# A hybrid decoder layer: output projection's tiles in four steps, FFN's first sums on VectorE, gate weight splits spread over the down projection

## The chip, the cores and the metric

One core of a Trainium2 chip runs the whole layer. The time is device microseconds of one execution, from launch to the output in memory. Lower is better. A time stands for the median of several executions; the profile is of one further execution.

Names used below: TensorE (PE) does matmuls and transposes, VectorE (DVE) and ScalarE (ACT) elementwise work, GpSimd (POOL) elementwise work too, and SyncE (SP) issues nearly all transfers, in one queue. On-chip memory is cut into two areas, mem_r (72 units, for operands of matmuls) and mem_f (30 units, for everything else); a unit is 512 floats in each of 128 partitions. PSUM has 8 banks of the same size.

## What is computed

The reference is a decoder layer for 1024 tokens of width 1024, in float32. Cut to what matters here:

```python
h = rmsnorm(x, mix_pre_norm)
z = h @ w_in
a = mla(z[..., :o1], z[..., o1:o2], z[..., o2:o3], ...)      # 8 heads, causal
c = short_gated_conv(z[..., o3:o4], z[..., o4:o5], z[..., o5:], conv_w)
m = concatenate([rmsnorm(a, attn_group_norm), rmsnorm(c, conv_group_norm)])
x = x + rmsnorm(m @ w_out, mix_post_norm)                    # output projection
h = rmsnorm(x, ffn_pre_norm)
f = (silu(h @ w_gate) * (h @ w_up)) @ w_down                 # FFN, width 2816
x = x + rmsnorm(f, ffn_post_norm)
e = rmsnorm(p @ w_ple_proj, ple_norm)
x = x + sigmoid(x @ w_ple_gate) * e                          # gate
```

## The kernel before

**Arithmetic.** Every float32 operand of a matmul is split into a high part (a cast on ScalarE, line 197) and a low part (the operand less its high part, on VectorE, line 198). A product is then three matmuls: high by high, high by low, low by high (lines 208 to 210, 1123 to 1126, 1281 to 1283). The three large products of FFN and of the gate use a scheme with seven block products in place of eight: blocks of the operands are first added to and subtracted from one another, then split, and seven products are summed into four blocks. The order of the seven is ORDER = 1, 2, 6, 5, 7, 3, 4. On the side of the activations the right operands are B11, B21 and B22 (plain blocks of the normed rows) and T1 to T4 (sums of blocks). Products 1 and 2 need B11 and B21 alone, which come from the first four row tiles.

**Output projection** (wo_a, lines 999 to 1019). There are eight tiles of 128 tokens. The convolution's half of the product, y, was stored to memory before (wo_c, line 941). For a tile, wo_a loads the rows of x and of y (lines 1001, 1002), makes the attention half with 24 matmuls into two banks (wo_half), adds y (line 1004), squares on ScalarE with a sum (line 218), adds epsilon on VectorE (line 214) and takes the power -1/2 on GpSimd (line 215), multiplies by that and the gain (line 1010), adds x (line 1011; on GpSimd in tiles 2, 4 and 6, by XP), stores the new residual row x1 (line 1013), and does the same norm once more into a third buffer, n1 (lines 1015 to 1017). Then h2_turn (line 1028) transposes n1 on TensorE, 8 transposes into 2 banks, copies them on ScalarE, and splits them: both halves for the first four tiles (B11, B21), one for the last four (B22). For the first four tiles the plain transposed copy is stored to memory too (hr_d, line 1048); for the last four it stays on the chip as tr[0] and tr[1]. The loop (line 1185) writes wo_a(t) and behind it h2_turn(t-1). The buffers of two units come from the first 22 units of mem_f (ML), of which the weights loaded ahead (line 1180) take two buffers.

**Start of FFN** (lines 1189 to 1223). FF is cut in 11 pairs of 128 columns each, fp; m is 0 for w_gate and 1 for w_up. `factor(fp, m, p)` (line 1082) makes the weight's operand for product p: for p = 6, 5, 7 and 3 of blocks that GpSimd adds (lines 1093, 1094, 1099, 1102), and splits it. `product` (line 1113) does the 12 matmuls and brings the result out of PSUM. The first four products (fp 0, p 1 and 2, m 0 and 1) are written around the last transposes; then the T's are made: lines 1206 and 1207 on VectorE, lines 1208 and 1216 on GpSimd, each 128x2048, each followed by a cast and a split of that size; then the products 1 and 2 of fp 1, and the loop over the rest, in which factor runs five products ahead (AHEAD). w_factors (line 1165) makes sums of w_down for the next stage on GpSimd.

**Down projection** (lines 1411 to 1434). 77 steps: f_load (two blocks), f_split (two splits), down (12 matmuls). Meanwhile wg_factors(k) (line 1302) prepares w_ple_gate: for each of four k two loads of 512 KB, seven splits and four GpSimd sums, called whole at four steps, 22, 17, 12 and 7 ahead of the last eleven.

**What sets the order.** The program is written as one sequence; a planner (the last lines, schedule_with_timeline_sim) then orders each engine's instructions, with modelled times and the written order as priority, and sets the waits. Each engine runs its own queue in that order. Buffers are chosen when the program is written: of those that are free, the one freed longest ago. A transfer into a buffer waits for the last reader of it.

Of the kernel before, what the change touches and what calls it, by code (L numbers as in the profile page):

```python
# [132 lines left out]
def hybrid_layer(ctx: ExitStack, tc: tile.TileContext, x, x_t, p_t, cols_in, positions,  # L133
# [36 lines left out]
    RG = ((56, 72),)  # L170
    ML, MG, MW = ((0, 22),), ((18, 22),), ((0, 8),)
# [759 lines left out]
    x1n = {}  # L931
# [66 lines left out]

    def wo_a(t):
        xr, y = mf(2, ML), mf(2, ML)  # L1000
        sp.dma_start(xr.a, x[t * P : (t + 1) * P, :])
        sp.dma_start(y.a, y_d[t * P : (t + 1) * P, :])
        ids, b = wo_half(t, mTa, 0)
        dve.scalar_tensor_tensor(y.a, b, ss_a[:, t : t + 1], y.a, op0=ALU.mult, op1=ALU.add)  # L1004
# [5 lines left out]
        dve.scalar_tensor_tensor(y.a, y.a, r, g_mix.a, op0=ALU.mult, op1=ALU.mult)  # L1010
        (pool if t in XP else dve).tensor_tensor(y.a, y.a, xr.a, op=ALU.add)
# [5 lines left out]
        dve.scalar_tensor_tensor(n1.a, y.a, r, g_ffn.a, op0=ALU.mult, op1=ALU.mult)
        free(y)
        x1n[t] = n1
# [8 lines left out]
    def h2_turn(t):  # L1028
        src = x1n.pop(t)
# [149 lines left out]

    raw_load(0, 0, MW)  # L1180
    for p in (1, 2):
        for m in range(2):
            factor(0, m, p)
    tr[0], tr[1] = mf(4, ((22, 26),)), mf(4, ((26, 30),))
    for t in range(T):
        wo_a(t)
        if t > 0:
            h2_turn(t - 1)
    for d in (mTa, wo):
        for h, l in d.values():  # L1190
            free(h, l)
    free(g_mix, g_ffn)
    head = [(0, m, p) for p in (1, 2) for m in range(2)]
# [302 lines left out]
```

## Time and profile before

| | |
|---|---|
| runs before | 1266.06, 1266.36 and 2819.84 us; median 1266.36 |
| profiled execution | 1260.9 us, span on the core 1259.1 us |
| mean granted TensorE clock | 0.986 |
| busy: PE, DVE, ACT, POOL | 1205.3, 823.3, 586.8, 544.6 us |
| moved by DMA | 215.68 MB, mean 171 GB/s |
| stages in the span | attention and what comes before it to about 440 us; output projection to 527; FFN's first products to 955; down projection, then the gate to the end |

The third run of those before stands alone, and the median is not moved by it. In the page, a group of instructions has its line, engine and operation, what it writes and reads, how often it ran, its busy time and the mean of one in ns. A row of the timeline gives start and length in us, and in brackets how long the engine stood idle before it and what ended that. In the busy time by stretch, PE's column is matmuls (their ends are modelled, they overlap), and the granted clock is 1.00 at full speed and 0.50 at half.

### The profile page before, as it was taken

What the parts mean: (1) busy time and instruction counts of PE and PEld (TensorE: products, weight loads), DVE (VectorE), ACT (ScalarE), POOL (GpSimd) and SP (SyncE); (2) the same over time, 40 slices, a digit from 0 to 9 for tenths busy, and PEclk for the clock granted to TensorE, in tenths of its full rate; (3) what the DMA queues carried; (4) which work ended last, traced back from release to release, by engine and by line L of the source; (5) the groups of instructions that cost most, each with busy time, mean ns of one, the idle gap of its engine ahead of it and who ended that gap; (6) DMA issues with size and microseconds to landing.
All of it is one profiled execution on the core that took longest, in us unless ns stands there. A gap on an engine that the chain in (4) does not pass through costs nothing.

```text
span 1259.1 us, 16644 instructions
## 1 busy us (share of the span) xinstructions
PE 1205.3 (96%) x5902; PEld 1012.9 (80%) x5902; DVE 823.3 (65%) x1158; ACT 586.8 (47%) x1071; POOL 544.6 (43%) x404
## 2 busy tenths in 40 slices
PE   7899999999999998769999999999999999989998
PEld 6898888888999886548888888888887888768886
DVE  7955457388867566697575564756535454889775
ACT  6542423277766644543333343333334445566552
POOL 5523544235634222277965665766611000442321
PEclk9999999999999998879999999999999999999999
DMA  7523554994541846435644445543337665566332
GB/s 244 171 67 109 184 185 162 285 336 115 137 104 56 284 161 209 159 109 184 234 163 143 147 157 184 176 167 139 137 126 277 199 190 186 180 222 234 118 128 82
DMA packets 88943, 215.68 MB, mean 171 GB/s; under 512 B 8920, under 2 KB 17404, under 8 KB 87548
## 3 DMA queue, kind: packets, MB, share of 16 engines
q1 hardware_dynamic: 88800, 214.60, 51.5%
q8 instruction: 46, 0.75, 0.3%
q14 instruction: 39, 0.30, 0.1%
q10 hardware_dynamic: 58, 0.02, 0.0%
HBM read 143.28 MB, written 71.04 MB: 170 GB/s over the span
## 4 chain that ended last, share of the span: by engine, by line
PE 80%; DVE 8%; DMA 6%; issue 2%; ACT 2%; POOL 1%; SPq 0%; DVEq 0%; ACTq 0%; POOLq 0%
PE banks L1125 11%; PE banks L1123 11%; PE banks L1126 11%; PE banks L208 7%; PE banks L210 7%; PE banks L209 7%; DVE mem_r L198 4%; PE banks L1282 4%; PE banks L1281 4%; PE banks L1283 4%; PE banks L843 2%; PE banks L1384 2%; PE banks L1381 2%; PE banks L1383 2%; PE banks L814 1%
## 5 line engine op out<-in xcount | busy, mean ns | idle before, releaser
L198 DVE TENSOR_TENSOR mem_r<-mem_f,mem_r 128x512 fp32r<-128x512 f32 (+3 forms) x401 | 397.1, 1019 | 211.9 <-ACT mem_r L197 200.0
L197 ACT CAST mem_r<-mem_f 128x512 fp32r<-128x512 f32 (+1 forms) x404 | 258.7, 669 | 402.5 <-PE banks L1125 160.9
L1123 PE MATMUL banks<-mem_r 128*128 128x512 f32 x616 | 244.0, 397 | 10.6 <-DVE mem_f L1004 7.0
L1125 PE MATMUL banks<-mem_r 128*128 128x512 f32 x616 | 243.6, 396 | 8.7 <-DVE mem_r L198 8.7
L1126 PE MATMUL banks<-mem_r 128*128 128x512 f32 x616 | 243.2, 395 | 0.0
L208 PE MATMUL banks<-mem_r 128*128 128x512 f32 (+2 forms) x536 | 196.3, 373 | 4.6 <-DVE mem_f L1004 3.3
L209 PE MATMUL banks<-mem_r 128*128 128x512 f32 (+2 forms) x536 | 197.1, 369 | 1.0 <-DVE mem_r L201 0.7
L210 PE MATMUL banks<-mem_r 128*128 128x512 f32 (+2 forms) x536 | 196.5, 368 | 0.0
L1123 PEld LDWEIGHTS banks<-mem_r 128*128 128x128 f32 x616 | 118.0, 191 | 37.2 <-issue 7.4
L1125 PEld LDWEIGHTS banks<-mem_r 128*128 128x128 f32 x616 | 117.8, 191 | 34.1 <-DVE mem_r L198 9.6
L1126 PEld LDWEIGHTS banks<-mem_r 128*128 128x128 f32 x616 | 117.9, 191 | 25.2
L1282 PE MATMUL banks<-mem_r 128*128 128x512 f32 x308 | 120.7, 392 | 7.5 <-DVE mem_r L198 7.5
L1281 PE MATMUL banks<-mem_r 128*128 128x512 f32 x308 | 119.2, 390 | 1.2 <-ACT mem_r L197 1.2
L1283 PE MATMUL banks<-mem_r 128*128 128x512 f32 x308 | 119.0, 389 | 0.0
L208 PEld LDWEIGHTS banks<-mem_r 128*128 128x128 f32 x536 | 100.9, 190 | 22.0 <-DVE mem_f L1004 3.9
L209 PEld LDWEIGHTS banks<-mem_r 128*128 128x128 f32 x536 | 101.6, 190 | 17.5 <-DVE mem_r L201 1.2
L210 PEld LDWEIGHTS banks<-mem_r 128*128 128x128 f32 x536 | 101.3, 189 | 16.3
L828 POOL TENSOR_TENSOR mem_f<-mem_f,stats 128x640 f32<-128x640 f32 (+5 forms) x64 | 72.5, 1147 | 92.6 <-DVE stats L827 46.7
L1141 DVE TENSOR_TENSOR mem_f<-banks,mem_f 128x512 f32<-128x512 f32 x66 | 45.3, 687 | 67.0 <-PE banks L1126 66.8
L215 POOL TENSOR_TENSOR small<-small,mhalf 128x1 f32<-128x1 f32 (+2 forms) x42 | 39.1, 930 | 114.6 <-DVE small L214 112.0
L198 DVE TENSOR_TENSOR mem_r<-banks,mem_r 128x512 fp32r<-128x512 f32 (+3 forms) x118 | 69.2, 611 | 10.5 <-ACT mem_r L197 9.7
L1282 PEld LDWEIGHTS banks<-mem_r 128*128 128x128 f32 x308 | 57.8, 188 | 22.0 <-DVE mem_r L198 10.4
(190 smaller groups left out, 1910.4 us busy)
## 6 DMA issues: line engine op xcount, KB each, us to landing
sc_d<-mem_f SPq DMA_DIRECT2D x77, 256.0 KB, 3.1
mem_f<-sc_d SPq DMA_DIRECT2D x77, 256.0 KB, 2.8
mem_f<-in_w_up_dram SPq DMA_DIRECT2D x22, 512.0 KB, 4.1
mem_f<-in_w_gate_dram SPq DMA_DIRECT2D x22, 512.0 KB, 4.6
mem_f<-in_w_down_dram SPq DMA_DIRECT2D x22, 512.0 KB, 4.6
wc_d<-mem_f SPq DMA_DIRECT2D x22, 512.0 KB, 3.0
mem_f<-wc_d SPq DMA_DIRECT2D x44, 256.0 KB, 2.8
mem_f<-in_w_down_dram SPq DMA_DIRECT2D x33, 256.0 KB, 3.9
```

Of the source, the lines that this page charges most:

```text
L197: act.copy(h, src)
L198: (eng or dve).tensor_tensor(l, src, h.bitcast(F32), op=ALU.subtract)
L208: pe.matmul(o, wh, vh, start=i == 0, stop=False)
L209: pe.matmul(o, wh, vl, start=False, stop=False)
L210: pe.matmul(o, wl, vh, start=False, stop=i == n - 1)
L828: pool.tensor_tensor(pt.a[:, 0:n], pt.a[:, 0:n], sm.to_broadcast([P, n]), op=ALU.mult)
L1123: pe.matmul(b, wh.a[:, c], th[:, k], start=first and k == 0, stop=False, skip_group_check=True)
L1125: pe.matmul(b, wh.a[:, c], tl[:, k], start=False, stop=False, skip_group_check=True)
L1126: pe.matmul(b, wl.a[:, c], th[:, k], start=False, stop=k == 3, skip_group_check=True)
L1281: pe.matmul(b, ah.a[:, c], bh.a, start=first, stop=False, skip_group_check=True)
L1282: pe.matmul(b, ah.a[:, c], bl.a, start=False, stop=False, skip_group_check=True)
L1283: pe.matmul(b, al.a[:, c], bh.a, start=False, stop=last, skip_group_check=True)
```

## The change

1. wo_a is cut in four: wo_a (product, sum with y, first square), wo_x1 (first norm, residual add, store of x1, second square), wo_n (second norm), h2_turn. The loop writes, for step t, wo_a(t), wo_x1(t-1), load of x(t), wo_n(t-2), h2_turn(t-3), load of y(t+2). The second norm writes into the row of y itself; the squares go to a buffer in mem_r; n1 is gone. The residual add is on VectorE for all tiles. The four head products are written in steps 8 and 9, their weight factors in step 4.
2. The sums for the T's and, for fp 0, the sums in factor are on VectorE. They are written in the order in which products use them, each T with its split directly behind its sum, between the products that come ahead of it.
3. raw_load of the second half of a pair's weights is written earlier, when the pair before has freed its own.
4. wg_factors becomes a generator (wg_steps) that yields after each piece; every second step of the down projection from step 4 on takes one piece.

```diff
+    def load_y(t):
+        rows_y[t] = mf(2, ML)
+        sp.dma_start(rows_y[t].a, y_d[t * P : (t + 1) * P, :])
...
+    def row_norm(t, i):
+        r = ss_y[:, 2 * t + i : 2 * t + i + 1]
+        junk = mr(2, BJ)
+        mean_sq(junk.a, rows_y[t].a, D, r)
+        free(junk)
+        rstd_of(r)
+
     def wo_a(t):
-        xr, y = mf(2, ML), mf(2, ML)
-        sp.dma_start(xr.a, x[t * P : (t + 1) * P, :])
-        sp.dma_start(y.a, y_d[t * P : (t + 1) * P, :])
+        y = rows_y[t].a
         ids, b = wo_half(t, mTa, 0)
...
+        row_norm(t, 0)
+
+    def wo_x1(t):
+        y, xr = rows_y[t].a, rows_x.pop(t)
+        dve.scalar_tensor_tensor(y, y, ss_y[:, 2 * t : 2 * t + 1], g_mix.a, op0=ALU.mult,
+                                 op1=ALU.mult)
+        dve.tensor_tensor(y, y, xr.a, op=ALU.add)
         free(xr)
...
+        sp.dma_start(x1_d[t * P : (t + 1) * P, :], y)
+        row_norm(t, 1)
+
+    def wo_n(t):
+        y = rows_y[t].a
+        dve.scalar_tensor_tensor(y, y, ss_y[:, 2 * t + 1 : 2 * t + 2], g_ffn.a, op0=ALU.mult,
+                                 op1=ALU.mult)
...
     def factor(fp, m, p):
+        eng = pool if fp else dve
...
+    for t in range(T + 3):
+        if t < T:
+            wo_a(t)
+        elif t == T:
...
+            for i in head[:2]:
+                product(*i)
+        elif t == T + 1:
+            for i in head[2:]:
+                product(*i)
+        if 1 <= t <= T:
+            wo_x1(t - 1)
+        if t < T:
+            load_x(t)
+        if 2 <= t <= T + 1:
+            wo_n(t - 2)
+        if t == T + 1:
+            free(g_mix, g_ffn)
+            raw_load(1, 0, ML)
+            b11 = mf(4, MG)
+            sp.dma_start(four(b11), hr_d[:, 0:4, :])
+        if t >= 3:
+            h2_turn(t - 3)
+        if t + 2 < T:
+            load_y(t + 2)
+        if t == T // 2:
+            for i in head:
+                factor(*i)
...
+    raw_load(0, 1)
+    dve.tensor_tensor(b12.a, b22.a, b12.a, op=ALU.subtract)
+    both(factor, 1, 1)
+    both(product, 1, 1)
+    dve.tensor_tensor(b11.a, b12.a, b11.a, op=ALU.add)
+    t_split("T2", b11)
+    both(factor, 1, 2)
+    both(product, 1, 2)
+    both(factor, 0, 6)
+    dve.tensor_tensor(b22.a, b22.a, b11.a, op=ALU.subtract)
+    t_split("T1", b22)
...
+    both(factor, 0, 5)
+    t_split("T3", b12)
...
+    dve.tensor_tensor(b21.a, b21.a, b11.a, op=ALU.subtract)
+    t_split("T4", b21)
...
-            if p == 6 and m == 0:
-                if fp > 0:
-                    raw_load(fp, 1)
             factor(fp, m, p)
+            if p == ORDER[-1] and m == 1 and fp + 1 < NP:
+                raw_load(fp + 1, 1)
...
+    wg_gen = (None for k in range(4) for _ in wg_steps(k))
...
-        if j in (-22, -17, -12, -7):
-            wg_factors((j + 22) // 5)
+        if i >= 4 and j < -2 and i % 2 == 0:
+            next(wg_gen, None)
```

More of the change, by code (lines that the diff above doesn't have):

```diff
@@ L170, in hybrid_layer @@
     RG = ((56, 72),)
+    BJ = ((32, 64),)
     ML, MG, MW = ((0, 22),), ((18, 22),), ((0, 8),)
@@ L1092, in factor @@
             if p == 6:
-                pool.tensor_tensor(a21, a21, a22, op=ALU.add)
-                pool.tensor_tensor(a11, a21, a11, op=ALU.subtract)
+                eng.tensor_tensor(a21, a21, a22, op=ALU.add)
+                eng.tensor_tensor(a11, a21, a11, op=ALU.subtract)
                 src = a11
@@ L1178, in w_factors @@
         free(*w)
+    load_y(0)
+    load_y(1)
     raw_load(0, 0, MW)
-    for p in (1, 2):
-        for m in range(2):
[L1183 to L1193, printed above, removed]
-    raw_load(1, 0, MW)
-    for i in head[:2]:
-        product(*i)
@@ L1197, in hybrid_layer @@
-    h2_turn(T - 1)
-    b11 = mf(4, MG)
-    sp.dma_start(four(b11), hr_d[:, 0:4, :])
-    for i in head[2:]:
-        product(*i)
-    for p in (1, 2):
-        for m in range(2):
-            factor(1, m, p)
-    b12, b22 = tr[0], tr[1]
-    dve.tensor_tensor(b12.a, b22.a, b12.a, op=ALU.subtract)
-    dve.tensor_tensor(b11.a, b12.a, b11.a, op=ALU.add)
-    pool.tensor_tensor(b22.a, b22.a, b11.a, op=ALU.subtract)
-    for n, v in (("T2", b11), ("T1", b22), ("T3", b12)):
+    tr[0], tr[1] = mf(4, ((22, 26),)), mf(4, ((26, 30),))
@@ new lines, in hybrid_layer @@
+    head = [(0, m, p) for p in (1, 2) for m in range(2)]
+    for t in range(T + 3):
+        if t < T:
+            wo_a(t)
+        elif t == T:
+            for d in (mTa, wo):
+                for h, l in d.values():
+                    free(h, l)
+            for i in head[:2]:
[21 more added lines that the diff above has]
+                factor(*i)
@@ L1210, in hybrid_layer, with both, t_split @@
+    b12, b22 = tr[0], tr[1]
+    def both(f, fp, p):
+        for m in range(2):
+            f(fp, m, p)
+    def t_split(n, v):
         h, l = tf[n] = pair(4, BT)
         split(h.a, l.a, v.a)
-        if n != "T2":
-            free(v)
+    raw_load(0, 1)
[6 more added lines that the diff above has]
+    both(product, 1, 2)
@@ L1214, in hybrid_layer @@
+    both(factor, 0, 6)
+    dve.tensor_tensor(b22.a, b22.a, b11.a, op=ALU.subtract)
+    t_split("T1", b22)
+    free(b22)
     b21 = mf(4, ((22, 26), (26, 30)))
     sp.dma_start(four(b21), hr_d[:, 4:8, :])
-    pool.tensor_tensor(b21.a, b21.a, b11.a, op=ALU.subtract)
-    h, l = tf["T4"] = pair(4, BT)
-    split(h.a, l.a, b21.a)
+    both(factor, 0, 5)
+    t_split("T3", b12)
+    free(b12)
+    factor(0, 0, 7)
+    dve.tensor_tensor(b21.a, b21.a, b11.a, op=ALU.subtract)
+    t_split("T4", b21)
@@ L1219, in hybrid_layer @@
     free(b11, b21)
-    for p in (1, 2):
-        for m in range(2):
-            product(1, m, p)
-    raw_load(0, 1)
     seq = [(fp, m, p) for fp in range(NP) for p in ORDER for m in range(2)
```

54 lines of the change are left out of this document (25 added, 29 removed).

## The prediction

> **What bounds the kernel now.** I read the page first, for the busy shares and the granted clock by slice.
>
> ```profile
> PE 1205.3 (96%) x5902; PEld 1012.9 (80%) x5902; DVE 823.3 (65%) x1158; ACT 586.8 (47%) x1071; POOL 544.6 (43%) x404
> ...
> PEclk9999999999999998879999999999999999999999
> ```
>
> TensorE is the bound, and no part of the change removes a matmul. So all that can be won is time in which TensorE stands still or runs at the lower clock. The next view, busy time by stretch, shows where that is. The columns are us, then busy time and count of PE, PEld, DVE, ACT and POOL, granted clock, DMA share, GB/s.
>
> ```profile
> 440.00:475.80 35.80, 35.80 (x175) 29.72 (x173) 22.93 (x31) 14.71 (x28) 7.84 (x9) 1.00 0.50 171
> 475.80:515.00 39.20, 28.73 (x112) 22.68 (x113) 25.01 (x30) 19.94 (x36) 10.03 (x10) 0.83 0.61 202
> 515.00:537.20 22.20, 17.10 (x74) 13.07 (x72) 17.81 (x17) 10.98 (x17) 9.69 (x6) 0.92 0.37 130
> 537.20:565.00 27.80, 18.15 (x55) 13.47 (x56) 26.58 (x14) 11.03 (x16) 21.46 (x9) 0.69 0.30 105
> 565.00:955.00 390.00, 390.00 (x1722) 322.96 (x1721) 231.79 (x247) 140.46 (x243) 245.95 (x166) 1.00 0.48 164
> ...
> 1060.00:1140.00 80.00, 72.46 (x312) 57.74 (x311) 66.10 (x84) 46.47 (x84) 25.62 (x16) 1.00 0.61 203
> ```
>
> The FFN's first products (565 to 955) are full. TensorE idles 10.47 us in the output projection (475.8 to 515), 5.10 us at its end, 9.65 us at the start of FFN and 7.54 us in the down projection. The clock falls to half six times between 486 and 562. The same view over these six stretches alone (three of them, and the sum):
>
> ```profile
> 527.23:530.64 3.41, 3.34 (x10) 2.37 (x9) 3.12 (x3) 1.56 (x3) 0.28 (x1) 0.50 0.95 321
> 537.47:551.12 13.65, 7.19 (x16) 4.96 (x16) 13.65 (x7) 5.29 (x8) 13.65 (x6) 0.50 0.24 80
> 557.95:561.36 3.41, 3.41 (x10) 2.64 (x9) 3.41 (x5) 0.75 (x2) 0.95 (x1) 0.50 0.99 332
> sum 34.13, PE 24.84 PEld 18.52 DVE 29.61 ACT 14.08 POOL 19.39; mean PE 4.14 PEld 3.09 DVE 4.94 ACT 2.35 POOL 3.23
> ```
>
> 24.84 us of matmul at half clock would take 12.42 at full clock; the last two of the six stretches hold 7.19 + 3.41 = 10.60 of it (5.30 lost), the first four 14.24 (7.12 lost). What stops TensorE is read in the timeline, engine by engine (start, us, what ran, and in brackets the idle time before it and what ended that).
>
> ```profile
> 476.98 0.50 PE L208 MATMUL banks<-mem_r 128*128 128x512 f32 x1 [1.18 <-DVE mem_f L1004]
> ...
> 509.51 0.77 PE L1123 MATMUL banks<-mem_r 128*128 128x512 f32 x1 [4.54 <-DVE mem_f L1004]
> ...
> 526.44 1.26 PE L1038 MATMUL banks<-ident,mem_f 128*128 128x128 f32 x8 [2.43 <-DVE mem_f L1017]
> ...
> 545.18 1.22 PE L1125 MATMUL banks<-mem_r 128*128 128x512 f32 x2 [5.55 <-DVE mem_r L198]
> 556.83 0.50 PE L1125 MATMUL banks<-mem_r 128*128 128x512 f32 x1 [3.12 <-DVE mem_r L198]
> ```
>
> In the projection it waits for the sum of the two halves (L1004), which itself waits for the tile's row of y, loaded too late:
>
> ```profile
> 484.37 1.28 DVE L1004 SCALAR_TENSOR_TENSOR mem_f<-banks,small,mem_f 128x1024 f32<-128x1024 f32 x1 [2.28 <-DMA mem_f<-y_d]
> ...
> 500.41 3.41 DVE L1017 SCALAR_TENSOR_TENSOR mem_f<-mem_f,small 128x1024 f32<-128x1024 f32 x1 [0.43 <-POOL small L215]
> ...
> 508.08 1.28 DVE L1004 SCALAR_TENSOR_TENSOR mem_f<-banks,small,mem_f 128x1024 f32<-128x1024 f32 x1 [3.97 <-DMA mem_f<-y_d]
> ```
> ```profile
> 500.34 2.40 POOL L1011 TENSOR_TENSOR mem_f<-mem_f 128x1024 f32<-128x1024 f32 x1
> ```
> ```profile
> 503.88 0.32 SPq L1002 DMA_DIRECT2D mem_f<-y_d  x1
> ```
>
> The last load of y is issued at 503.88, just after the L1017 that began at 500.41 has ended (503.82): it waited for a buffer. That L1017 took 3.41 us beside GpSimd's add of 2.40 us. At the start of FFN, TensorE waits for splits behind sums that GpSimd makes:
>
> ```profile
> 538.02 4.96 POOL L1208 TENSOR_TENSOR mem_f<-mem_f 128x2048 f32<-128x2048 f32 x1
> ```
> ```profile
> 528.35 2.29 DVE L1206 TENSOR_TENSOR mem_f<-mem_f 128x2048 f32<-128x2048 f32 x1 [0.29 <-ACT mem_f L1042]
> ...
> 539.14 9.35 DVE L198 TENSOR_TENSOR mem_r<-mem_f,mem_r 128x2048 fp32r<-128x2048 f32 x3
> 548.41 1.76 DVE L1145 TENSOR_TENSOR mem_f<-mem_f 128x512 f32<-128x512 f32 x1
> ```
> ```profile
> 543.01 1.90 ACT L197 CAST mem_r<-mem_f 128x2048 fp32r<-128x2048 f32 x1 [4.22 <-POOL mem_f L1208]
> ```
>
> A sum of 128x2048 takes 4.96 us on GpSimd and 2.29 on VectorE, and while GpSimd works VectorE's own splits stretch (three in 9.35).
>
> **Projection in four steps.** Per tile nothing is computed less; the third buffer (n1) goes, since both norms are now in place and the squares are written to the area of the matmul operands, and y is loaded two tiles ahead. Counting double buffers (11 in the area, 2 taken by the first gate and up weights): five rows of y, one of x and one transposed copy live at the worst point, two left over. So the wait for a buffer before a y load should go. What then sets the pace? By rows of the stretch 440 to 565:
>
> ```profile
> L218 ACT ACTIVATE mem_f<-mem_f 128x1024 f32<-128x1024 f32 x16 | 17.0, 1060 | 31.5 <-POOL mem_f L1011 11.8 <-DVE mem_f L1004 10.0 <-DVE mem_f L1011 9.7
> ...
> L215 POOL TENSOR_TENSOR small<-small,mhalf 128x1 f32<-128x1 f32 (+1 forms) x17 | 11.3, 664 | 54.6 <-DVE small L214 54.6
> ...
> L1010 DVE SCALAR_TENSOR_TENSOR mem_f<-mem_f,small 128x1024 f32<-128x1024 f32 x8 | 10.2, 1281 | 2.7 <-POOL small L215 2.6
> ...
> L198 DVE TENSOR_TENSOR mem_r<-banks,mem_r 128x512 fp32r<-128x512 f32 x12 | 8.1, 684 | 0.7 <-ACT mem_r L197 0.6
> ...
> L1011 DVE TENSOR_TENSOR mem_f<-mem_f 128x1024 f32<-128x1024 f32 x5 | 6.1, 1220 | 0.1
> ...
> L214 DVE TENSOR_SCALAR small<-small 128x1 f32<-128x1 f32 (+1 forms) x17 | 2.6, 151 | 7.6 <-ACT mem_f L218 7.4
> ```
> ```profile
> 516.98 1.03 PE L1038 MATMUL banks<-ident,mem_f 128*128 128x128 f32 x8
> ```
>
> VectorE per tile: three passes of 1.28, an add of 1.22 (tiles 2, 4 and 6 come over from GpSimd), two of 0.15, and two splits of 0.68 in tiles 0 to 3, one after: 6.73 and 6.05 us. TensorE per tile: 24 matmuls at 390.00/1722 = 0.227, and 1.03 of transposes: 6.47. Over eight tiles 51.1 on VectorE, plus the four splits of the first gate and up factors that move in at tile 4 (2.7), against 51.8 on TensorE, which has four products of 12 (10.9) to follow. VectorE is a 2 us lag at most. The waits within a tile (square 1.06, power 0.66) lie a tile apart and are covered.
>
> Each moved DMA counts: in tiles 3 to 6 a step issues a load of y, one of x, a store of x1 and a store of the transposed copy, 4 x 0.524 MB in 6.6 us = 318 GB/s. The two stretches above with the DMA engines at 0.95 and 0.99 moved 321 and 332. So for four tiles the queue is as good as full, and landings are long already:
>
> ```profile
> mem_f<-y_d SPq DMA_DIRECT2D x8, 512.0 KB, 5.8
> x_d<-mem_f SPq DMA_DIRECT2D x8, 512.0 KB, 3.4
> ...
> hr_d<-mem_f SPq DMA_DIRECT2D x4, 512.0 KB, 5.7
> ```
>
> A new wait is added: the ffn pass now overwrites y, so VectorE must wait until the store of x1 from it has landed (3.4 us median). Queued behind it on VectorE are the splits that TensorE's next products need, and the next tile's pass. The step between store and pass is 6.5 us, so it is hidden unless the store waits in SP's queue behind a load. I give back 1 us for each of the four DMA-full tiles and 2 for VectorE's lag: 6 us, between 0 and the whole 22.7 us lost there now (15.57 idle, 7.12 clock).
>
> **FFN's first sums on VectorE.** A moved sum of 128x512 costs 0.68 (the split of that size) to 1.76 us (L1145 beside GpSimd); with GpSimd left with powers I take 0.68. After the last transposes the products of fp 1 that need only the first half (48 matmuls, 10.9 us) cover: difference 2.29, sum 2.29, cast 1.90, split taken at 2.29 (same size and operands; 9.35 if it stretched as above) = 8.8. But also four weight splits, four moved sums and two splits of product 6, and three result passes stand there, 13 x 0.68 = 8.8, on VectorE: 6.9 + 8.8 = 15.7 in all, 13.0 if only the first half of product 6 must precede. Stall 2 to 5, I take 3. T1, T3, T4 then need about 4.6 each against 5.4 us of products. Of the 14.95 us lost from 537.2 on (9.65 idle, 5.30 clock) 12 come back; bounds 0 and 14.95. The second half's raw weights are now loaded before the sums; later loads move only within the stretch with TensorE at 390.00 of 390, worth nothing.
>
> **Gate weights over the down projection.** Now four bursts of seven splits each:
>
> ```profile
> 1072.52 13.95 DVE L198 TENSOR_TENSOR mem_r<-mem_f,mem_r 128x512 fp32r<-128x512 f32 x16 [0.31 <-ACT mem_r L197]
> ```
> ```profile
> 1098.68 0.50 PE L1282 MATMUL banks<-mem_r 128*128 128x512 f32 x1 [2.05 <-DVE mem_r L198]
> ```
>
> Afterwards one split and at most one GpSimd sum come with every second step of 12 x 0.227 = 2.72 us. VectorE needs 2 x 0.68 + 0.68, at 0.87 each beside GpSimd (13.95/16) 2.6, and only every second step: it fits. 7.0 of 7.54 come back; bounds 0 and 7.54.
>
> **Sum.** 22.7 - 6 + 12 + 7 = 35.7, less about 3 for clock lost on the gaps that remain. In this trace 2.43 us of idle (before 526.44) was followed by half clock at 527.23, while 2.05 us (before 1098.68) was not, so a small gap costs nothing or another 1.7 us (half of 3.41). Hence 32.7. The profiled execution took 1260.9 us (span 1259.1); 1260.9 - 32.7 = 1228.2. The median of the runs shown is 1266.36, 5.5 above it, so I forecast 1234.
>
> [...]
>
> **Rivals.**
> 1. *DMA paces the projection.* For: 318 against 321 to 332 GB/s. Against: only four tiles, and two are loaded early. If landings of 5.8 stretch the step to 8 us for all eight tiles, 8 x 1.5 = 12 instead of 6, plus clock on each gap (4 x 1.7, less the 3): about 10 more, 1244.
> 2. *VectorE becomes the bound at FFN's start.* GpSimd's weight sums of the first pair begin while T3 and T4 are split, as L1216 does now; four splits at 4.7 (half of 9.35) instead of 2.29 cost 9.6, plus 3 of clock: 1246. Against: T4 isn't needed until four product pairs later.
> 3. *The order written is not the order run.* The program is re-ordered by modelled times: L1017 of tile 7 stands behind products that are written after it. If the tiles already run as far apart as data allow, only sums and spread count: 12 + 7 - 3 = 16, 1250. Against: the buffer that the y load waited for is a matter of storage, not order.
> 4. *Slower.* A load of y that waits for a buffer stands in SP's queue ahead of the store of x1; VectorE waits for that store in the in-place pass; the transposes that free the buffer come behind it. One turn is store 3.4, pass 1.28, transposes 1.03, y load 5.8, then sum, square, power, pass, add (1.28 + 1.06 + 0.66 + 1.28 + 1.22): 17.0. It decides once fewer than 1.4 tiles pass in a turn of 17.0: then a step is over 12 us, 8 x 5.6 = 45, all that can be won. At 13 us a step: 1266.4 - 45.2 + 8 x 6.5 = 1273. Against: two buffers are left over, so four tiles should pass in a turn.
>
> **How the numbers follow.** Forecast 1234: 0.55 (1222 to 1240). Rival 1: 0.2; rival 2: 0.12; rival 3: 0.08; rival 4: 0.05. The best case is 1266.4 - 45.2 = 1221. Leaving out the slowest rival and the edges, the range is 1222 to 1256. A measurement of this kernel can tell about 2% from no change, so faster means below 1241: the forecast nearly whole, under half of rival 1 and a little of rival 2: 0.63. Within 2%: 0.32. Slower: 0.05.
>
> **What would show it.** Right: no y load ends a wait of the row sum; TensorE's idle between 475 and 540 under 6 us; the clock at half for under 10 us in place of 34; the products from T2 on start some 25 us earlier than 537; gaps in the down projection under 1 us. Wrong: VectorE's ffn pass waiting for the store of x1, SP's issues of y still late, VectorE's large splits over 4 us, or a gap before every second down step.

## The result, and the profile after

The kernel after took 1235.62 us (median of four, 1233.22 to 1239.15) against 1266.9 on the same chip: 0.9758 of the time before, 95% interval 0.9722 to 0.9793. The forecast was 1234, faster. The profiled execution took 1233.22 us against 1260.9, 27.7 less, where the forecast's sum had 32.7.

The page first: busy shares, and the granted clock by slice.

```profile
PE 1194.3 (97%) x5902; PEld 1008.5 (82%) x5902; DVE 816.9 (66%) x1171; ACT 586.1 (48%) x1071; POOL 518.0 (42%) x391
...
PEclk9999999999999999989999999999999999999999
```

TensorE issues the same 5902 instructions; one slice shows a lower clock where there were three. Busy time by stretch (columns as before):

```profile
440.00:475.80 35.80, 35.80 (x177) 29.96 (x175) 26.97 (x36) 14.39 (x27) 7.91 (x9) 1.00 0.59 193
475.80:500.00 24.20, 24.20 (x119) 19.92 (x118) 22.08 (x28) 17.09 (x34) 5.18 (x6) 1.00 0.81 267
500.00:512.50 12.50, 10.56 (x55) 8.68 (x55) 11.28 (x19) 7.90 (x14) 2.06 (x2) 1.00 0.68 237
512.50:545.00 32.50, 21.27 (x83) 16.47 (x82) 27.29 (x22) 15.73 (x20) 8.03 (x3) 0.79 0.26 89
545.00:930.00 385.00, 385.00 (x1701) 318.88 (x1700) 230.78 (x248) 140.30 (x243) 248.38 (x166) 1.00 0.48 165
930.00:1035.00 105.00, 100.86 (x437) 82.69 (x436) 72.20 (x95) 57.71 (x104) 20.34 (x13) 0.98 0.68 228
1035.00:1130.00 95.00, 95.00 (x425) 78.77 (x424) 67.49 (x100) 49.16 (x89) 9.92 (x7) 1.00 0.67 222
```

The output projection is full up to 500. The start of FFN (512.5 to 545) still is not, and there the mean granted clock is 0.79. In the down projection the gaps of the four bursts are gone (95.00 of 95.00), but two new ones stand at its start. The timeline of TensorE shows all five gaps, each with what ended it:

```profile
502.83 1.06 PE L1056 MATMUL banks<-ident,mem_f 128*128 128x128 f32 x8 [1.94 <-ACT mem_f L1162]
521.91 1.22 PE L1142 MATMUL banks<-mem_r 128*128 128x512 f32 x2 [6.19 <-ACT mem_r L198]
528.17 1.22 PE L1142 MATMUL banks<-mem_r 128*128 128x512 f32 x2 [5.04 <-ACT mem_r L198]
```
```profile
940.34 0.50 PE L1320 MATMUL banks<-mem_r 128*128 128x512 f32 x1 [2.51 <-ACT mem_r L198]
950.25 0.50 PE L1321 MATMUL banks<-mem_r 128*128 128x512 f32 x1 [1.63 <-DVE mem_r L199]
```

And the two stretches at half clock, in place of six:

```profile
518.47:532.13 13.66, 5.18 (x11) 3.51 (x12) 13.66 (x11) 4.84 (x4) 4.61 (x1) 0.50 0.17 58
941.73:945.14 3.41, 3.41 (x10) 2.66 (x9) 3.41 (x5) 3.41 (x7) 1.51 (x1) 0.50 0.67 217
sum 17.07, PE 8.59 PEld 6.17 DVE 17.07 ACT 8.25 POOL 6.12; mean PE 4.29 PEld 3.09 DVE 8.54 ACT 4.12 POOL 3.06
```

8.59 us of matmul at half clock lose 4.3, where 24.84 lost 12.4, if half of it is counted as lost. In the second of the two stretches matmuls start 0.43 us apart, at full clock 0.23, so the half is a little high.

Why the start of FFN still waits is read on VectorE and ScalarE. The second norms of the last two tiles (L1036), then the two sums toward T2 and the split of T2 (L199 is the split, L198 the cast; the first of the two casts in each ScalarE row is that of T2, then of T1):

```profile
501.40 1.28 DVE L1036 SCALAR_TENSOR_TENSOR mem_f<-mem_f,small 128x1024 f32<-128x1024 f32 x1
...
505.61 1.28 DVE L1036 SCALAR_TENSOR_TENSOR mem_f<-mem_f,small 128x1024 f32<-128x1024 f32 x1
...
513.64 2.28 DVE L1245 TENSOR_TENSOR mem_f<-mem_f 128x2048 f32<-128x2048 f32 x1
...
517.64 2.28 DVE L1248 TENSOR_TENSOR mem_f<-mem_f 128x2048 f32<-128x2048 f32 x1
...
521.65 2.28 DVE L199 TENSOR_TENSOR mem_r<-mem_f,mem_r 128x2048 fp32r<-128x2048 f32 x1
```
```profile
519.96 2.42 ACT L198 CAST mem_r<-mem_f 128x2048 fp32r<-128x2048 f32 x2 [2.01 <-DVE mem_f L1248]
526.22 2.42 ACT L198 CAST mem_r<-mem_f 128x2048 fp32r<-128x2048 f32 x2 [3.85 <-DVE mem_f L1253]
```

The gap of 1.94 us ends with a row of ScalarE in this view, but the transposes behind it read the row that L1036 finished at 502.68; in run 7 below, where this part of the kernel is the same, the gap at this place (2.19 us) is put down to L1036. So it is taken here as the wait for a tile's norm.

Every sum takes 2.28 us, where 2.29 was forecast. But the row of the last tile was ready at 506.9, and its transposes ran only at 511.49 to 512.53: TensorE's queue had put most of the 48 matmuls of the second pair, the cover for this chain, ahead of them. Only 3.2 us of the 10.9 were left (512.53 to 515.72), then 6.19 us of gap until T2's cast. Behind product 6's first matmuls TensorE's queue holds one that waits for T1 (cast from 526.22 on), so the first of product 5, ahead of the rest of product 6, for which T2's split was there at 523.93: the second gap, 5.04.

Last, the wait that the change adds, VectorE's in-place pass (L1036) waiting for the store of x1, and the one wait for a row of y that is left (L1021):

```profile
455.06 1.28 DVE L1036 SCALAR_TENSOR_TENSOR mem_f<-mem_f,small 128x1024 f32<-128x1024 f32 x1 [0.39 <-DMA x_d<-mem_f]
468.88 1.28 DVE L1036 SCALAR_TENSOR_TENSOR mem_f<-mem_f,small 128x1024 f32<-128x1024 f32 x1 [1.67 <-DMA x_d<-mem_f]
486.69 1.28 DVE L1021 SCALAR_TENSOR_TENSOR mem_f<-banks,small,mem_f 128x1024 f32<-128x1024 f32 x1 [0.42 <-DMA mem_f<-y_d]
```

None of the three moves TensorE, which is full there.

### The profile page after: what moved, and what is told of

Read it like the earlier page. It is cut to its first block, busy times and chain, and to the rows that moved or that the text cites. A ratio compares the mean times of both kernels' runs of the same rounds, so it can differ in the third digit from the quotient of the medians.

```text
span 1231.2 us, 16627 instructions
## 1 busy us (share of the span) xinstructions
PE 1194.3 (97%) x5902; PEld 1008.5 (82%) x5902; DVE 816.9 (66%) x1171; ACT 586.1 (48%) x1071; POOL 518.0 (42%) x391
## 4 chain that ended last, share of the span: by engine, by line
PE 88%; DVE 5%; DMA 3%; ACT 2%; issue 2%; POOL 0%; SPq 0%; ACTq 0%; DVEq 0%; POOLq 0%
PE banks L1142 11%; PE banks L1144 11%; PE banks L1145 11%; PE banks L209 7%; PE banks L211 7%; PE banks L210 7%; PE banks L1321 5%; PE banks L1322 5%; PE banks L1320 5%; PE banks L844 2%; PE banks L1430 2%; PE banks L1427 2%; PE banks L1429 2%; DVE mem_r L199 2%; PE banks L815 2%
## 5 line engine op out<-in xcount | busy, mean ns | idle before, releaser
L199 DVE TENSOR_TENSOR mem_r<-mem_f,mem_r 128x512 fp32r<-128x512 f32 (+2 forms) x401 | 382.8, 983 | 204.9 <-ACT mem_r L198 196.2
L198 ACT CAST mem_r<-mem_f 128x512 fp32r<-128x512 f32 (+2 forms) x404 | 258.6, 670 | 385.4 <-PE banks L1144 152.1
L1142 PE MATMUL banks<-mem_r 128*128 128x512 f32 x616 | 240.9, 392 | 11.2 <-ACT mem_r L198 11.2
L1142 PEld LDWEIGHTS banks<-mem_r 128*128 128x128 f32 x616 | 116.1, 189 | 36.3 <-ACT mem_r L198 12.4
L1144 PEld LDWEIGHTS banks<-mem_r 128*128 128x128 f32 x616 | 116.0, 188 | 24.6 <-DVE mem_r L199 0.7
L1145 PEld LDWEIGHTS banks<-mem_r 128*128 128x128 f32 x616 | 116.1, 188 | 24.1
L210 PEld LDWEIGHTS banks<-mem_r 128*128 128x128 f32 x536 | 101.4, 189 | 17.0 <-DVE mem_r L202 1.2
L209 PEld LDWEIGHTS banks<-mem_r 128*128 128x128 f32 x536 | 100.6, 189 | 17.9 <-ACT mem_r L198 1.1
L211 PEld LDWEIGHTS banks<-mem_r 128*128 128x128 f32 x536 | 101.2, 189 | 16.2
L199 DVE TENSOR_TENSOR mem_r<-banks,mem_r 128x512 fp32r<-128x512 f32 (+3 forms) x118 | 69.1, 611 | 10.5 <-ACT mem_r L198 9.8
L198 ACT CAST mem_r<-banks 128x512 fp32r<-128x512 f32 (+3 forms) x118 | 58.8, 537 | 25.0 <-PE banks L844 13.7
```

The source lines that it names most:

```text
L198: act.copy(h, src)
L199: (eng or dve).tensor_tensor(l, src, h.bitcast(F32), op=ALU.subtract)
L209: pe.matmul(o, wh, vh, start=i == 0, stop=False)
L210: pe.matmul(o, wh, vl, start=False, stop=False)
L211: pe.matmul(o, wl, vh, start=False, stop=i == n - 1)
L1142: pe.matmul(b, wh.a[:, c], th[:, k], start=first and k == 0, stop=False, skip_group_check=True)
```

## The experiments

All were timed beside the kernel before, whose medians were then 1263.1 to 1264.9 us. The table puts the losses of TensorE of each profiled execution in three places: the projection up to the start of the last tile's transposes, FFN from there, and the down projection. In each: idle time plus what half clock cost (half the matmul time in half-clock stretches). Both are sums over the trace's matmul records; the row of the kernel after can be added up from the rows above. The column "441 to FFN's end" is the length from the end of the matmuls that sum columns, at about 441 us, to the last matmul of FFN's first products.

Two things limit how closely these rows can be compared. The kernel after was timed beside a kernel before of 1266.9 us, the others beside quicker ones, so a difference from it comes out up to 3 us otherwise by medians than by ratios. And each trace is one execution: runs 3 and 7 don't touch the stretch from 441 to FFN's end, and it took 486.1 and 488.6 us there, 485.2 in the kernel after.

| kernel | median (range), us | ratio [95%] | projection | FFN | 441 to FFN's end | down: length, losses |
|---|---|---|---|---|---|---|
| before | 1266.9 | 1 | 13.1 + 5.5 | 12.1 + 7.0 | 508.5 | 222.6, 8.8 + 0 |
| after | 1235.6 (1233.2 to 1239.2) | 0.9758 [0.9722, 0.9793] | 1.9 + 0 | 11.2 + 2.6 | 485.2 | 217.8, 4.1 + 1.7 |
| 1 four steps only | 1253.9 (1253.2 to 1254.2) | 0.9920 [0.9903, 0.9936] | 3.3 + 1.6 | 17.7 + 4.3 | 496.6 | 228.2, 11.8 + 3.4 |
| 2 sums on GpSimd | 1246.8 (1245.7 to 1249.7) | 0.9868 [0.9852, 0.9884] | 3.5 + 2.9 | 16.2 + 4.9 | 497.4 | 218.0, 4.4 + 1.7 |
| 3 bursts | 1244.8 (1241.3 to 1250.1) | 0.9852 [0.9824, 0.9880] | 2.1 + 0 | 11.2 + 3.2 | 486.1 | 227.3, 10.2 + 3.4 |
| 4 low part first | 1237.6 (1236.1 to 1239.0) | 0.9785 [0.9768, 0.9801] | 4.4 + 0 | 13.3 + 1.7 | 488.6 | 218.0, 4.4 + 1.7 |
| 5 cover behind transposes | 1231.7 (1230.8 to 1233.9) | 0.9741 [0.9726, 0.9757] | 5.7 + 0 | 3.4 + 2.7 | 481.9 | 218.8, 4.9 + 1.7 |
| 6 storage only | 1255.0 (1249.7 to 1255.5) | 0.9920 [0.9898, 0.9942] | 8.1 + 3.4 | 10.0 + 3.1 | 495.3 | 227.1, 10.1 + 3.4 |
| 7 spread late | 1232.6 (1229.7 to 1235.4) | 0.9746 [0.9724, 0.9767] | 3.1 + 1.6 | 11.2 + 2.9 | 488.6 | 213.3, 1.6 + 0 |
| 8 the edits of 4, 5 and 7 | 1229.4 (1227.9 to 1230.5) | 0.9719 [0.9701, 0.9737] | 6.0 + 0 | 3.1 + 4.4 | 483.1 | 213.7, 2.0 + 0 |
| 9 storage and sums | 1250.0 (1247.4 to 1251.3) | 0.9893 [0.9877, 0.9910] | 7.8 + 3.4 | 8.5 + 2.6 | 492.9 | 224.4, 9.0 + 1.7 |
| 10 the edits of 5 and 7 | 1229.5 (1226.1 to 1230.5) | 0.9720 [0.9700, 0.9741] | 6.7 + 0 | 4.2 + 3.2 | 484.4 | 215.5, 2.3 + 1.5 |
| 11 and last norm first | 1230.3 (1229.2 to 1231.1) | 0.9737 [0.9721, 0.9754] | 4.9 + 0 | 5.7 + 4.7 | 485.1 | 213.7, 1.9 + 0 |
| 12 and norm in a buffer apart | 1230.2 (1226.1 to 1231.6) | 0.9726 [0.9703, 0.9750] | 1.2 + 0 | 8.9 + 1.6 | 482.4 | 217.8, 3.6 + 2.7 |

**1. The projection in four steps alone.** The kernel after, with the sums, their order, the loads of the weights' second halves and the bursts as before.

```diff
-        eng = pool if fp else dve
+        eng = pool
...
+    pool.tensor_tensor(b22.a, b22.a, b11.a, op=ALU.subtract)
...
+    pool.tensor_tensor(b21.a, b21.a, b11.a, op=ALU.subtract)
...
+    raw_load(0, 1)
...
-        if i >= 4 and j < -2 and i % 2 == 0:
-            next(wg_gen, None)
+        if j in (-22, -17, -12, -7):
+            wg_factors((j + 22) // 5)
```

> The projection in four steps as in the changed kernel; the sums of FFN's start (engine and order) and the bursts of the gate weights as before. Theory: the four steps carry most of the gain, since TensorE's idle in the projection falls from 15.6 to about 2 us and the half clock there goes: some 21 us, 1244 to 1249 us. Rival, the recorded sum: the projection gives 16.7 less the clock of its remaining gaps, and the sums another 12: this kernel then takes about 1252 us.

Measured: 1253.9 us, 0.9920 of before, some 10 us: near the rival's 1252, not the theory's. The projection's loss falls from 18.6 to 4.9, so this part does in its own place what was forecast. But FFN's losses grow from 19.1 to 22.0 and the down projection's length from 222.6 to 228.2. TensorE reaches the same sums earlier and stands before them longer:

```profile
503.37 1.94 PE L1056 MATMUL banks<-ident,mem_f 128*128 128x128 f32 x8 [3.22 <-DVE mem_f L1036]
...
524.50 1.22 PE L1142 MATMUL banks<-mem_r 128*128 128x512 f32 x2 [6.74 <-ACT mem_r L198]
...
530.51 1.22 PE L1142 MATMUL banks<-mem_r 128*128 128x512 f32 x2 [4.78 <-ACT mem_r L198]
...
537.90 0.80 PE L1144 MATMUL banks<-mem_r 128*128 128x512 f32 x1 [6.18 <-DVE mem_r L199]
```

**2. The sums back on GpSimd.** The kernel after, but for:

```diff
-        eng = pool if fp else dve
+        eng = pool
...
-    dve.tensor_tensor(b22.a, b22.a, b11.a, op=ALU.subtract)
+    pool.tensor_tensor(b22.a, b22.a, b11.a, op=ALU.subtract)
...
-    dve.tensor_tensor(b21.a, b21.a, b11.a, op=ALU.subtract)
+    pool.tensor_tensor(b21.a, b21.a, b11.a, op=ALU.subtract)
```

> The changed kernel with the sums of fp 0 and of T1 and T4 back on GpSimd, in the new order. Theory: FFN's start stalls anyway (13.8 us of 14.95 remain in the changed kernel), so the engine is worth little: the same, up to 5 us more (1235 to 1241 us). Rival, the recorded sum: the engine is what brings 12 us, so this takes 1245 us or more.

Measured: 1246.8 against 1235.6 for the kernel after, intervals apart; the theory fell and its rival came out. So the engine of the sums is worth 11.2 us by medians and 13.9 by ratios once the projection is quick, and the 12 of the forecast stands as the price of undoing this part. (The theory set 13.8 us, counted from the last transposes, against 14.95, counted from 537.2; by one cut FFN's losses are 13.8 against 19.1.) With run 1 this also parts the engine from the order: with the sums on GpSimd the stretch to FFN's end is 496.6 us in the old order and 497.4 in the new one, so the order alone brings nothing that shows. The sum toward T1 takes 6.56 us on GpSimd, against 2.28:

```profile
524.58 6.56 POOL L1253 TENSOR_TENSOR mem_f<-mem_f 128x2048 f32<-128x2048 f32 x1
```

**3. The bursts back.** The kernel after with wg_factors called whole at four steps.

```diff
-        if i >= 4 and j < -2 and i % 2 == 0:
-            next(wg_gen, None)
+        if j in (-22, -17, -12, -7):
+            wg_factors((j + 22) // 5)
```

> The changed kernel with the gate weights' splits in four bursts as before. Theory: from the first matmul of the down projection to its last, the changed kernel is 4.8 us shorter than before, because a new stall of 4 us at the start of that stage eats part of the 7.5 that the bursts cost; with bursts the stage takes 222.5 us again and the kernel 1239 to 1241. Rival: the new stall at the start has nothing to do with the gate weights and stays: 1243 or more.

Measured: 1244.8 against 1235.6, intervals apart: 9.2 us by medians, 11.9 by ratios, and 9.5 in the down projection (227.3 against 217.8). The rival's time came out, but not its reason: at the stage's start one gap of 1.51 us is left of the 2.51 and 1.63. What the theory missed is that the same bursts cost more here than in the kernel before: 10.2 idle and 3.4 of clock against 8.8 and 0. What the records show of the clock's share stands at the end. Of the 9.5 us, 7.8 are such losses; where the other 1.7 went is open.

**4. The low part first.** In product, high by low is issued ahead of high by high, so that the first matmul of product 5 waits with the others for T1's split.

```diff
-            pe.matmul(b, wh.a[:, c], th[:, k], start=first and k == 0, stop=False,
+            pe.matmul(b, wh.a[:, c], tl[:, k], start=first and k == 0, stop=False,
...
-            pe.matmul(b, wh.a[:, c], tl[:, k], start=False, stop=False, skip_group_check=True)
+            pe.matmul(b, wh.a[:, c], th[:, k], start=False, stop=False, skip_group_check=True)
```

> The changed kernel; in each FFN product the high part of the weight meets the low part of the activations first, then the high part (same matmuls, other order). Theory: the second stall at FFN's start (5.04 us) is the planner's order on TensorE, which puts the first matmul of product 5 (it needs T1's cast) ahead of the rest of product 6, whose split was there 4.2 us earlier. With the low part first that can't be: some 4 us of idle and 1 to 2 of half clock go, 1229 to 1232 us. Rival: T1's chain sets the pace in any case, the stall only moves behind product 6: 1235.

Measured: 1237.6, nothing won, and the theory fell. The two gaps became one that ends with a split at 533, though T2's split had ended at 527.97:

```profile
533.03 0.79 PE L1142 MATMUL banks<-mem_r 128*128 128x512 f32 x1 [13.25 <-DVE mem_r L199]
```

**5. The cover behind the transposes.** The four products of the second pair may be issued only behind the last transpose.

```diff
-    both(product, 1, 1)
+    with tc.issue_after(last_turn[0].ins):
+        both(product, 1, 1)
...
-    both(product, 1, 2)
+    with tc.issue_after(last_turn[0].ins):
+        both(product, 1, 2)
```

> The changed kernel; the four products 1 and 2 of fp 1 are queued on TensorE behind the transposes of the last tile. Theory: the cover that the prediction counted on (10.9 us between the last transposes and the first product that needs T2) was used up ahead of the transposes, so T2's chain of 8.3 us lay open by 6.2; with the cover in its place the last transposes come up to 4 us earlier, and the stall of 6.2 shrinks to the 3 us or so for which TensorE waits for the last tile's norm: 1229 to 1233 us. Rival: TensorE idles as long ahead of the transposes as it did behind them: 1235 or more.

Measured: 1231.7, as the theory had it. In the trace the cover now covers: FFN's losses fall from 13.8 to 6.1 us. Half of that comes back ahead of the transposes, where TensorE now waits for the norms themselves:

```profile
504.61 1.06 PE L1058 MATMUL banks<-ident,mem_f 128*128 128x128 f32 x8 [2.29 <-DVE mem_f L1036]
508.82 1.94 PE L1058 MATMUL banks<-ident,mem_f 128*128 128x128 f32 x8 [3.14 <-DVE mem_f L1036]
```

The time is 3.9 us under that of the kernel after by medians and 2.2 by ratios, and the intervals overlap. So the mechanism rests on the trace: the stretch to FFN's end is 481.9 us, under all three traces of the kernels with the old order of this part (485.2, 486.1 and 488.6).

**6. Storage alone.** The kernel before, its tiles still in two steps; the second norm writes into y, the squares go to the operand area, n1 is gone. The weights loaded ahead of the second pair may use the whole row area.

```diff
-        n1 = mf(2, ML)
...
-        mean_sq(n1.a, y.a, D, r)
+        junk = mr(2, BJ)
+        mean_sq(junk.a, y.a, D, r)
+        free(junk)
...
-        dve.scalar_tensor_tensor(n1.a, y.a, r, g_ffn.a, op0=ALU.mult, op1=ALU.mult)
-        free(y)
-        x1n[t] = n1
+        dve.scalar_tensor_tensor(y.a, y.a, r, g_ffn.a, op0=ALU.mult, op1=ALU.mult)
+        x1n[t] = y
```

> The kernel before, with the second norm in place and the squares written to the matmul operands' area (no third buffer), but the steps of a tile still written one behind the other, and nothing else changed. Theory: the loads of y were late for want of a buffer, so storage alone takes most of the projection's waits away: 1246 to 1252 us. Rival: the distance between the steps is what counts, since the second norm and the transposes of a tile wait for its own chain: 1260 us or more.

Measured: 1255.0 us, 0.9920, between theory and rival, and the same as the four steps with their storage (run 1). The projection keeps 11.5 us of losses against 4.9, but FFN has 13.1 against 22.0. So on its own the distance between the steps is worth nothing in the end: what it saves is lost again before the sums. The forecast's third rival said that the written order would bring nothing here; that holds as long as the sums are slow.

**9. Storage and the sums.** Run 6 with the sums on VectorE in the order of the kernel after. It parts the distance from the sums.

```diff
+        eng = pool if fp else dve
...
-    pool.tensor_tensor(b22.a, b22.a, b11.a, op=ALU.subtract)
...
+    dve.tensor_tensor(b11.a, b12.a, b11.a, op=ALU.add)
+    t_split("T2", b11)
+    both(factor, 1, 2)
+    both(product, 1, 2)
+    both(factor, 0, 6)
+    dve.tensor_tensor(b22.a, b22.a, b11.a, op=ALU.subtract)
+    t_split("T1", b22)
```

> The kernel before with the in-place second norm and the squares in the operand area (as in the run of the storage alone), and the sums at FFN's start on VectorE in order of use; tiles still in two steps, gate weights still in bursts. Theory, storage and sums are what pays and the four steps add nothing: the stage from the sums of columns to FFN's last product falls from 495.3 (storage alone) by the 10.5 to 12.2 that the sums gave beside the four steps, to 483 to 485, and the time is that of the kernel after with bursts, 1244.8 (1242 to 1248). Rival, the distance of a tile between the steps is needed once the sums are quick, because the last tile's rows come later without it: the stage stays over 489 and the time over 1249.

Measured: 1250.0, the rival's side. Without the four steps the sums win about 5 (from 1255.0), with them about 9 (run 1 to run 3, 1253.9 to 1244.8). Part of the 5 is the down projection, which neither edit touches; in the stretch to FFN's end the sums win 2.4 us without the steps (495.3 to 492.9) and 10.5 with them (496.6 to 486.1). Against run 3 the intervals just touch. The gaps that the four steps take away are these:

```profile
472.86 0.50 PE L209 MATMUL banks<-mem_r 128*128 128x512 f32 x1 [2.50 <-DVE mem_f L1005]
...
494.65 1.06 PE L1041 MATMUL banks<-ident,mem_f 128*128 128x128 f32 x8 [1.35 <-DVE mem_f L1021]
...
511.87 1.07 PE L1041 MATMUL banks<-ident,mem_f 128*128 128x128 f32 x8 [1.44 <-DVE mem_f L1021]
```

So the parts don't add up as separate terms: the distance pays only where the sums behind it are quick, and the sums pay more where the tiles arrive early. (The four steps of run 3 also hold the residual adds on VectorE and the weight factors at tile 4; their share wasn't parted.)

**7 and 8. The spread later, and all three edits.** The gate weights' pieces from step 12 on, in three of five steps, so that their loads don't stand in SP's queue among the first blocks of the down projection, as these two do in the kernel after:

```profile
933.19 0.33 SPq L1343 DMA_DIRECT2D mem_f<-in_w_ple_gate_dram  x1
...
934.54 0.43 SPq L1344 DMA_DIRECT2D mem_f<-in_w_ple_gate_dram  x1
```

```diff
-        if i >= 4 and j < -2 and i % 2 == 0:
+        if i >= 12 and j < -2 and i % 5 in (0, 2, 4):
```

> The changed kernel; the pieces of the gate weights begin at step 12 of the down projection in place of step 4, three in five steps. Theory: the two gaps at that stage's start (2.51 and 1.63 us, and a stretch of half clock) come from the first gate weight loads of 512 KB, which stand in SP's queue and on ScalarE ahead of the next steps' blocks: 3 to 5 us less, 1231 to 1233 us. Rival: the gap is there without them too (1.2 us before, 1.5 with bursts): at most 2 us less.

> The changed kernel with all three edits: low part first, cover behind the last transposes, gate weights from step 12. Theory: the gains add up but for 1 or 2 us, 1222 to 1227 us. Rival: the chain of the last tile's norm and T2 is as long as before and TensorE waits for it somewhere: 1230 or more.

Measured: 1232.6 and 1229.4. The down projection goes from 217.8 to 213.3 and 213.7 us. That takes away all but one of its gaps, and its half clock. Run 7 came out as its theory had it by median (3.0 us less), but by ratio it is 1.5 less and its interval overlaps that of the kernel after: the 4.5 us are the trace's, and ahead of this stage the same trace is 3.3 longer. In run 8 the gains did not add up: neither its theory's 1222 to 1227 nor quite its rival's 1230.

**10, 11 and 12. What holds the last transposes.** Run 10 has the edits of runs 5 and 7. Run 11 adds that VectorE's work for the second pair's factors and for product 6's factors stands behind the last norm; run 12, on top of that, that the norms of tiles 6 and 7 are written to a buffer apart.

```diff
-    both(factor, 1, 1)
...
+    with tc.issue_after(last_n[0].ins):
+        both(factor, 1, 1)
```
```diff
-        y = rows_y[t].a
+        y = rows_y[t]
+        if t >= 6:
+            rows_y[t] = mf(2, ML)
```

> The kernel after with the four products of the second pair behind the last transposes and the gate weights from step 12 on in three of five steps. Theory, the two edits are independent and the low part first adds nothing: 1231.7 less 3.0 is 1228.7, between 1227 and 1230. Rival, the low part first was worth something once the cover stands behind the transposes: 1231 or more, and a gap of over 2 us stays ahead of product 6.

> The run before this one, with VectorE's work for the second pair's factors and for product 6's factors put behind the last tile's second norm. Theory, that work in VectorE's queue holds the norm up and with it the last transposes: the norm starts some 3 us earlier than 507, the wait ahead of the last transposes falls from 3.1 to under 1.5 us with no half clock there, and the time is 1224 to 1226. Rival, the work comes out late in its turn: the products of the second pair or product 6 wait for their factors, and the time stays at 1228 to 1231.

> The run before this one (VectorE's work for the second pair behind the last norm), with the second norm of tiles 6 and 7 written to a buffer of its own instead of into y, so that it needn't wait for the store of x1. In the run before, those two norms began at 502.95 and 506.95 after waits of 1.40 and 1.31 us for that store, whose landing took 4.1 us and more beside the loads of the gate and up weights. Theory, with VectorE's queue cleared the store is what holds the last norm: the norms start by 502 and 504, the two gaps ahead of the last transposes (1.98 and 2.93) shrink to 2 us together, no half clock there, 3 to 6 us less: 1224 to 1227. Rival, what follows waits anyway (the first half's transposed copy, the factors put behind): the gap moves to product 5 or 6 and the time stays at 1228 to 1231.

Measured: 1229.5, 1230.3 and 1230.2. Run 10 came out as its theory had it; against run 8 it shows that the low part first adds nothing. Run 11's theory fell: with VectorE's queue cleared the norms stand still for the store of x1,

```profile
502.95 1.28 DVE L1038 SCALAR_TENSOR_TENSOR mem_f<-mem_f,small 128x1024 f32<-128x1024 f32 x1 [1.40 <-DMA x_d<-mem_f]
...
506.95 1.28 DVE L1038 SCALAR_TENSOR_TENSOR mem_f<-mem_f,small 128x1024 f32<-128x1024 f32 x1 [1.31 <-DMA x_d<-mem_f]
```

the wait that the in-place pass brings in. And the factors that were put behind come late: ahead of product 5 TensorE now waits 5.66 us for T1's cast (1.83 and 1.04 at this place in run 10). Run 12 takes the wait for the store away: the norms start at 501.03 and 503.04, and the projection's loss is down to 1.2 us. The wait for T1's cast is as long as in run 11:

```profile
523.66 1.65 PE L1151 MATMUL banks<-mem_r 128*128 128x512 f32 x3 [5.70 <-ACT mem_r L198]
```

The time stays, but not for the reason of the rival: up to FFN's end this trace is 2.7 us shorter than that of run 11 (482.4 against 485.1), and its down projection is 4.1 longer (217.8 against 213.7). There TensorE waits for a cast that waits for a load of w_down, and half clock follows (932.98 to 939.81):

```profile
934.45 2.08 PE L1334 MATMUL banks<-mem_r 128*128 128x512 f32 x4 [3.57 <-ACT mem_r L198]
```

That gap is 1.61, 2.04, 2.31 and 1.92 us in runs 7, 8, 10 and 11, all with the same spread of the gate weights. So the late spread doesn't remove it, and whether the norm apart wins something is open.

Runs 8 and 10 are the best versions, 1229.4 and 1229.5, by medians 6 us under the kernel after, by ratios 5; the intervals of their ratios and its own overlap at the ends.

## Why the prediction was right, and where its terms were off

**What bounds.** Right: no matmul went, and the 27.7 us come from idle time and clock. By the trace, the stretch from 441 to FFN's last product went from 508.5 to 485.2 us (23.3 less), the down projection from 222.6 to 217.8 (4.8), and the rest stayed.

**The projection: too careful.** "I give back ... 6 us": 1.94 were lost, with no half clock. The load of y and VectorE's lag, for which the 6 were set aside, cost TensorE nothing up to 500. From 475.8 to 500 the DMA engines were busy for 0.81 at 267 GB/s, and in the fullest stretch of a step's length (480.0 to 486.6) for 0.95 at 301, so the 318 GB/s of the forecast were nearly reached; but TensorE stayed full, and rival 1 is out. By the table's cut the projection's loss fell from 18.6 to 1.9. The forecast's 22.7 reaches to 537.2 and holds 4.1 us more, which the table counts to FFN.

**FFN's first sums: the step that failed.** "Stall 2 to 5, I take 3": two gaps of 6.19 and 5.04, and 2.6 of clock. The chain was sized about rightly: 8.8 forecast to the end of T2's split, 10.3 measured (513.64 to 523.93), of which 1.7 are smaller work of VectorE between the two sums. The cover was not. I counted all 10.9 us of the second pair's products behind the last transposes, but 3.2 stood there. Run 5 shows this: with all of them behind the transposes FFN's losses fall from 13.8 to 6.1, and 3.8 us more are lost ahead of the transposes, where the cover had stood. The second gap is the order of TensorE's queue, product 5's first matmul among product 6's. Rival 3 had the right mechanism, but for another place than the one where it mattered. So 12 were to come back here, and the place itself shows 5.3 (19.1 to 13.8). Undoing the part costs 11.2 (run 2), because without it 21 to 22 us would be lost in FFN behind the quicker projection, and in run 2 4.5 more ahead of it: the forecast added terms that depend on each other.

**The spread: about right, for a partly different reason.** 7 forecast, 4.8 found in place, 9.2 by undoing. The bursts' gaps did go. At the start of the down projection, where the kernel before has a gap of 1.23, there are now 2.51 and 1.63. The forecast costed the gate weights' loads at nothing; run 7 moves them and one gap of 1.61 is left, which isn't theirs.

**Clock.** 3 us were set aside for the gaps that remain; it was 4.3.

**The sum.** Idle and clock from 441 to FFN's end: forecast to fall by 25.7 (22.7 - 6 + 12 - 3), measured 21.9 by the table (37.7 to 15.8, before rounding). With the spread 2.2 short, and 1.3 us of the stage's gain outside these losses, the profiled execution came out 5.0 above the 1228.2 of the sum (3.8 + 2.2 - 1.3, and 0.2 from ahead of 441). The median stood 2.4 above the profiled execution, not 5.5; that made up for 3.1. That the time is right to 1.6 us is luck: errors that cancel.

**The slower rival.** Its wait exists (0.39 and 1.67 us on VectorE) and was covered, as argued against it. Run 11 shows that it is the next in line once the queue before it is shorter. VectorE's large splits took 2.28 and 2.29 us; rival 2 is out. Its price was read wrongly: the row of 9.35 us merges one split of 128x2048 (5.99) with two of 128x512 (1.76 each). The four splits of that size in the kernel before took 2.78, 5.99, 6.67 and 2.28, 4.4 in the mean, so that the 4.7 came out near by luck.

**What was to show it.** Half clock under 10 us: 17.07. TensorE idle under 6 between 475 and 540: 13.17. No y load ends a wait of the row sum: one did, 0.42. The products from T2 on some 25 us earlier than 537: the first came at 521.91, 15.4 earlier than 537.28; the last FFN product came 23.04 earlier (949.61 to 926.57). Gaps in the down projection under 1 us: 2.51 and 1.63. So all five signs of being right failed by their letter, while the time held. Of the signs of being wrong, the wait for the store of x1 showed; it cost TensorE nothing.

**Open.** Why the queue of TensorE comes out with product 5's first matmul among those of product 6 was not tried apart: run 4 changed what that matmul waits for, not its place. What sets the length of the gap at the start of the down projection (1.6 to 3.6 us in runs 7, 8, 10, 11 and 12) wasn't tried either.

## What to carry to other kernels

A cover counts only if it stands behind the wait in the queue of the engine that waits; ask where the planner will put it, and pin it there rather than trust the written order (run 5, where that won 2 to 4 us). When a stage in front is sped up, work out what the next stage's wait becomes before adding the two gains: here four steps alone won no more than storage alone, since the gap moved on. The length of a small gap on TensorE alone didn't give its price here: one of 2.16 us in run 9 was followed by half clock, one of 2.06 in the same trace and one of 2.05 in the kernel before were not (below).

## What the runs showed of the clock

The forecast left open why 2.43 us of idle was followed by half clock and 2.05 was not. All changes of clock lie on a grid of 3.41 us in each trace (in the kernels before and after the 16 changes from 430 to 1215 us, to within 0.01); counted from the start of the span, the grid lies elsewhere in each, in these two 1.49 us apart. Laying that grid over the records of TensorE of all fourteen kernels from 430 to 1215 us, I counted the full-clock windows that were idle for 0.8 us or more: of 41 with 1.91 us or more, all 41 were followed by a window at half clock; of 49 with less than 1.78, none; between, 2 of 6. In the kernels before and after alone it is 8 of 8 with 1.96 us or more, and none of 10 with 1.63 or less. In run 9, the bursts' gaps of 2.06 us (ending 1084.43) and 2.16 (ending 1101.20), each with the window after it:

```profile
1080.84:1084.25 3.41, 1.52 (x7) 0.94 (x5) 3.41 (x3) 2.32 (x5) 2.90 (x2) 1.00 0.11 41
1084.25:1087.67 3.42, 3.24 (x14) 2.67 (x15) 3.42 (x7) 0.74 (x2) 0.00 (x0) 1.00 0.67 213
1097.90:1101.31 3.41, 1.25 (x7) 0.71 (x6) 3.41 (x4) 2.34 (x5) 2.61 (x2) 1.00 0.34 90
1101.32:1104.73 3.41, 3.41 (x9) 2.67 (x10) 3.41 (x7) 1.21 (x3) 0.00 (x0) 0.50 0.75 249
```

Idle is the first column less PE's: after 1.89 in the window the clock stayed, after 2.16 it was half. In the kernel before, the gap of 2.05 us lay across a boundary:

```profile
1093.84:1097.25 3.41, 2.79 (x12) 1.95 (x11) 3.41 (x3) 2.81 (x6) 3.25 (x3) 1.00 0.29 103
1097.25:1100.66 3.41, 1.98 (x9) 1.64 (x10) 3.41 (x5) 1.47 (x3) 0.83 (x1) 1.00 0.28 71
1100.66:1104.07 3.41, 3.41 (x17) 2.79 (x15) 2.83 (x6) 1.90 (x4) 0.00 (x0) 1.00 0.97 341
```

0.62 and 1.43 us: no half clock followed. No window of the down projection in the kernel before was idle for more than 1.43 us (8.8 us idle in all, no clock lost); the same bursts in run 3 lost 3.4. The two gaps at FFN's start, 6.19 and 5.04 us in the kernel after, with 11.2 us idle there in it and in runs 3 and 7, cost 2.6, 3.2 and 2.9 us of clock. All this is a count over these traces; what sets the clock they don't show.
